# A hybrid decoder step on one core: three feature tiles at the opening, another order for the bias table's copies, wider value products and a later state store

## The chip, the core and the metric

The kernel runs on one core of one Trainium2 chip. A core has TensorE (PE, matrix products into PSUM), VectorE (DVE), ScalarE (ACT), GpSimd (POOL), and SyncE (SP), which here only issues transfers; the transfers themselves are carried by 16 DMA engines. Every engine runs its own instructions in the order in which they were written, and waits on semaphores for the others. The time is the device time of one execution in microseconds (us), given as the median of several runs.

## The reference

One layer of a decoder trunk for a prompt of 512 tokens and for 8 running sequences with one new token each. The input of 1024 columns is multiplied by one weight matrix of 3600 columns; the parts of the result feed two mixers:

```python
h = jnp.einsum('btd,de->bte', x, w_in)
qa, ka, va, za, ga, qb, kb, vb, gb = jnp.split(h, split_points, axis=-1)
log_a = jax.nn.log_sigmoid(jnp.einsum('btr,rk->btk', za, w_alpha2) + b_alpha) / GATE_TEMP
o_a, s_new = gla_chunked(qa * DK_A ** -0.5, ka, va, log_a, s0, chunk)  # S_t = diag(a_t) S_{t-1} + k_t^T v_t, o_t = q_t S_t
o_a = o_a * lax.rsqrt(jnp.mean(jnp.square(o_a), axis=-1, keepdims=True) + RMS_EPS) * gla_norm_g
o_b = prompt_dilated(qb, kb, vb, rel_bias)    # 8 heads; windows of 128, 512, 2048 at steps 1, 4, 16
mix = jnp.concatenate([o_a * jax.nn.silu(ga), o_b * jax.nn.silu(gb)], axis=-1)
x_new = layer_norm(DEEPNORM_ALPHA * x + mix @ w_out, ln_g, ln_b)
```

Mixer A (qa, ka, va, za, ga) is gated linear attention with four heads and a running state; mixer B (qb, kb, vb, gb) is attention over strided windows of keys with a bias by distance. Outputs are the new rows, the states and the new keys and values.

## The kernel before

**Precision and products.** All products of float32 numbers are made of three faster ones: each operand is split into a high part, rounded to the fast type by ScalarE (`hi`), and a rest, made by VectorE (`lo`); TensorE then adds hi·hi, hi·lo and lo·hi (`three`, lines 611 to 613). A feature tile is 128 columns of the weights against all 520 token columns, in two halves of 264 and 256, with 8 blocks of 128 rows: 48 products per tile.

**A planner writes the order.** The kernel is written as tasks (Python generators). `Plan` keeps a model of when each engine is free, with a cost for each operation (`Op`, lines 81 to 127), and always issues the operation that can start first in the model; between those that start together the task with the smaller priority number goes first (`PRIO`, line 70). The result is a fixed order of instructions on each engine. The chip then runs those orders with its own times. A transfer's cost in the model depends on its bytes, on the length of its runs and on the number of rows; all transfers that the model knows share one queue.

**Tiles.** `SLOTS` and `BANKS` name rings of buffers. The weights as loaded go into `r` (2 slots), the split weights into `w` (6 slots, so three pairs), most other things into `g` (27). PSUM has eight banks: three `d` for the feature and token products, three `s`, two `t`. A weight tile's load is issued when a slot in `r` comes free, that is when an earlier tile has been split; its split is placed as soon as a pair in `w` comes free.

**The opening** (`first_loads`, `first_splits` and the head of `dense`). The list `FIRST` (line 533) alternates blocks of x (128 rows of x, 266 KB; the first one in two halves) and blocks of the first weights, the 256 columns of ka0 and ka1. SP issues them in that order, ScalarE and VectorE split them, and TensorE multiplies block by block into four banks, so that it can work while x still arrives. Four small loads of the gate's second weights (`wz`) go over ScalarE's queue at the very start (`clear`). Behind the opening stands the product of x with the gate's first weights (`za`, line 705), and its logarithm and running sums (`gate_decay`, lines 747 to 783); then follow the features qa0, qa1, qb0 to qb3, kb0 to kb3, and on through `dense`.

**The bias table** (`bias_table`, lines 787 to 805). A product gives one row of 640 biases for each of 8 heads. The rows are stored to DRAM (`tab`), and then copied there 23 times per head into `tabr` [8, 23, 640] in one transfer from DRAM to DRAM (line 804), so that a tile of 128 rows, each shifted by one against the row above, can be read from it. These reads are the 16 `strip` loads (lines 1114 to 1127): row p of a strip is put together from two counters, 8 outer and 16 inner.

**Scores and values.** `softmax` adds the strip, makes the probabilities, turns them by TensorE and splits them; `weighted` (lines 1198 to 1226) multiplies them with the values. The value tile holds the high parts in its first 64 columns and the low parts in the next 64. For each block of keys there is one product of all 128 columns with the high probabilities, and one of the first 64 columns with the low ones.

**The levels of mixer A.** `gla_levels` (lines 808 to 855) makes, for seven block sizes, decayed copies of qa and ka (`d`, exponentials on ScalarE, `qs` and `ks` on VectorE), and `gla_level` their products (`ps_l`), two sizes together.

**The end.** The last products go to the rows of the last token block; then the state's last product, its copy by ScalarE and its store over ScalarE's queue (lines 950 to 957) stand beside the last layer norm (`norm(3)`, lines 1580 to 1615), which needs a chain of five small ScalarE steps between VectorE's statistics and its last pass over the rows.

Of the kernel before, what the change touches and what calls it, by code (L numbers as in the profile page):

```python
# [67 lines left out]


PRIO = dict(  # L70
    wload=3, wsplit=4, decay=10, res_s=8, res=8, level=22, keys_out=2, logit=50, value=20, fills=9, bias_table=7.3, gla_levels=15.3, gla_diagonal=7.7, gla_state=24, gla_queries=25, strips=14, sample_queries=48, sample_softmax=2.5, sample_values=46, sample_gla=11, mix_sample_a=8.7, mix_sample_b=16, ln_rows=17, keys_store=17.5, gla_out=26, sample_v=12, mix_tiles=33.5, scores=31, softmax=34.2, weighted=30, mix_a=18, mix_b=19, norm3=11, norm=9)
# [9 lines left out]
class Op:  # L81
# [3 lines left out]
    def __init__(self, eng, fn, args, kw):  # L85
# [13 lines left out]
        if fn == "dma_start":  # L99
            c = 640 if eng.name == "SP" else 100  # L100
# [93 lines left out]
class Plan:  # L194
# [11 lines left out]
    def pool(self, tag, n, pool):  # L206
        self.slots[tag] = [(pool, f"{tag}{i}", {}) for i in range(n)]
# [11 lines left out]
    def free(self, *xs):  # L219
        for x in xs:  # L220
            name = x.tensor.name
            self.shares[name] = self.shares.get(name, 1) - 1
            if self.shares[name] == 0:
                last = {}
                for (_, eng), end in self.uses.pop(name, {}).items():
                    last[eng] = max(last.get(eng, 0.0), end)
                tag, (pool, t, _) = self.slot_of.pop(name)
                self.slots[tag].append((pool, t, last))

    def alloc(self, need):  # L230
        for i, tag in enumerate(need.tags):
            slots = self.slots[tag]
            if len(slots) > (need.spare if i == len(need.tags) - 1 else 0):
                s = min(slots, key=lambda s: max(s[2].values(), default=0.0))
                slots.remove(s)
                pool, t, last = s
# [132 lines left out]
def trunk(ctx: ExitStack, tc: tile.TileContext, xT, xp, xs, state, ck, cv, w_in, wab, gnorm,  # L369
# [42 lines left out]
    def split(raw, hi, lo):  # L412

        yield S.copy(hi, raw)
        yield V.tensor_tensor(lo, raw, hi.bitcast(F32), op=ALU.subtract)
# [89 lines left out]
    order = [g for k, g in groups.items() if k not in ("ka0", "ka1")] + wo  # L505
# [29 lines left out]
    ka_raw = []  # L535

    def first_loads():
        za = w_in[:, OFF["za"]:OFF["za"] + 16].rearrange("(k p) n -> p k n", p=P)
        for n, a, *b in FIRST:
            if n == "x":  # L540
                c = b[0] if b else slice(0, NT)
                if a % 2 == 0 and c.start == 0:
                    xraw.append((yield Need("g", f"x_raw{a}", [P, 2, NT])))
                yield D.dma_start(xraw[a // 2][:, a % 2, c], xT[a * P:(a + 1) * P, c])
            else:
                if a % 4 == 0:
                    ka_raw.append((yield Need("r", f"raw_ka{a}", [P, 4, GW])))
                rows = w_in[a * P:b[0] * P, OFF["ka"]:OFF["ka"] + GW]
                yield D.dma_start(ka_raw[a // 4][:, a % 4:a % 4 + b[0] - a, :], rows.rearrange("(k p) n -> p k n", p=P))
            mark("first")  # L550
        yield D.dma_start(zw[:, :, :16], za)
        mark("zw")
# [8 lines left out]

    ka_hl = []

    def first_splits():
        for j, (n, a, *b) in enumerate(FIRST):
            yield At("first", j + 1)
            if n == "x":
# [6 lines left out]
                yield from split(xraw[a // 2][:, a % 2, c], xh[a][:, c], xl[a][:, c])  # L574
                mark("xs")
            else:
                if a % 4 == 0:
                    hl = []
                    for x in ("hi", "lo"):
                        hl.append((yield Need("w", f"{x}_ka{a}", [P, 4, GW], F32R)))  # L580
                    ka_hl.append(hl)
                    for i in range(2):
                        g = groups[f"ka{i}"]
                        for l, y in zip((g.hi, g.lo), hl):
                            l += [y[:, k, i * P:i * P + P] for k in range(4)]
                r = slice(a % 4, a % 4 + b[0] - a)
                yield from split(ka_raw[a // 4][:, r, :], *(y[:, r, :] for y in ka_hl[a // 4]))
                for _ in range(a, b[0]):
                    mark("kas")
                if b[0] % 4 == 0:  # L590
                    free(ka_raw[a // 4])
# [92 lines left out]
    def dense():  # L684
# [6 lines left out]
        for i in range(2):  # L691
            for u in range(2):
                pk[i, u] = yield bank("ds"[i], f"ps_ka{i}{u}")
        for k in range(KT):
            for u in range(2):
                yield At("kas", k + 1)
                yield At("xs", k + 1 + (u if k == 0 else 1))
                for i in range(2):
                    yield from three(pk[i, u][:, :TW[u]], k, halves(k, u, groups[f"ka{i}"]))
        for x in ka_hl:  # L700
            free(*x)

        pz = yield bank(("t", "s"), "ps_za")
        yield At("zw")
        yield Batch(T.matmul(pz[j * 32:j * 32 + 32, :QN[j]], zw[:, k, :], xraw[k // 2][:, k % 2, Q0[j]:Q0[j] + QN[j]],
                             start=k == 0, stop=k == KT - 1, skip_group_check=True)
                    for k in range(KT) for j in range(TT))
        free(zw, *xraw)
        add(gate_decay(pz), PRIO["decay"])
# [5 lines left out]
        for i in range(2):  # L715
            yield from feature(groups[f"qa{i}"], into("qa", qa_s, i, 0.125))
# [29 lines left out]

    def gate_decay(pz):
# [8 lines left out]
        la = yield Need("g", "la", [P, 2 * NP + 2 * NB])  # L756
# [9 lines left out]
        ls = la[:, 2 * NP:].rearrange("p (m b) -> p m b", m=2)  # L766
        parts_ = [(zv[j][:, :, :P], lv[:, :, j * P:j * P + P], lv[:, :, j * P:j * P + P]) for j in range(TT)]
        parts_.append((zv[1][:, :, P:], ls, la_s))
# [18 lines left out]
    def bias_table():  # L787
# [16 lines left out]
        yield D.dma_start(tabr, tab[:, None, :].to_broadcast([HB, T_R, T_P]))  # L804
# [97 lines left out]
    def gla_state():  # L902
# [51 lines left out]
        free(kt, B["va1"])  # L954
        yield S.copy(st[:, TT - 1].rearrange("p m v -> p (m v)"), ps[:, :256])
# [158 lines left out]
    def strips():  # L1114
        yield At("tab")
        yield At("qb", 1)
        for pi in range(2):
            w = 256 * (pi + 1)
            for h in range(HB):
# [6 lines left out]
                                                 ap=[[T_P - 16, 8], [T_P - 1, 16], [1, w]]))  # L1126
# [71 lines left out]
    def weighted(h, pi):  # L1198
# [12 lines left out]
        for k in range(last + 1):  # L1211
# [3 lines left out]
            yield T.matmul(pv[:64, o], vk[:, :64], ptl[:, k, o], start=False, stop=k == last, skip_group_check=True)  # L1215
# [364 lines left out]
    def norm(t):  # L1580
# [18 lines left out]
        if last:  # L1599
# [3 lines left out]
            yield S.activation(rstd, nt[:, 0:1], AF.Identity, scale=rstd)  # L1603
            yield from centre(cs[0])
# [20 lines left out]
    add(fills(), PRIO["fills"])  # L1625
    add(dense(), 100)
# [124 lines left out]
```

## Time and profile before

| | us |
|---|---|
| median of 3 runs | 289.97 |
| range of the runs | 289.93 to 292.68 |
| the profiled execution | 290.49 |
| its span, from the first to the last instruction | 288.6 |

The span of the profiled execution is 1.9 us shorter than its own time; what lies between is around the instructions. The busy times of the engines, the chain of waits and the rows of single instructions stand in the prediction, ahead of the sentences that use them. A row of a group reads: line, engine, operation, written tile, read tiles, shapes, count, then busy time and mean duration in ns, then the engine's idle time ahead and who ended it. All operations are recorded at one line (364, the planner's), so groups are told apart by the names of their tiles. In a row of a timeline the first number is the start, the second the duration, both in us. A row of the chain gives start, length and engine in the same way. A queue's row (SPq, ACTq) is the issue of a transfer, not its run; the transfers themselves are seen as the share of the 16 DMA engines and in GB/s.

### The profile page before, as it was taken

Reading aid. Unit: us, or ns where it says so; the run is one execution under the profiler, and the core shown is the slowest. Engines: PE = TensorE matmul, PEld = TensorE weight load, DVE = VectorE, ACT = ScalarE, POOL = GpSimd, SP = SyncE. Lnnn points to the kernel's source line nnn. Section 1 sums busy time; section 2 is a strip of 40 time slices with the busy share of each in tenths; the row PEclk is TensorE's granted clock in tenths of the full one; section 3 lists DMA queues with packets and bytes.
Section 4 is the critical chain, followed back from the end, with each engine's and each line's share of the span. In section 5 each row is a group of like instructions: output and inputs, shape, how many; then the busy total and the mean of one; then the engine's idle time right before and its main releaser. Section 6 shows DMA issues by size and latency. Waiting matters only on the chain.

```text
span 288.6 us, 6896 instructions
## 1 busy us (share of the span) xinstructions
PE 276.3 (96%) x2638; PEld 261.0 (90%) x2638; DVE 223.9 (78%) x549; ACT 168.9 (59%) x472; POOL 54.3 (19%) x74
## 2 busy tenths in 40 slices
PE   7999999999999999999999999999999969999990
PEld 4999999998999999898999999999999969997890
DVE  3837897999889879899899877756889594339845
ACT  5757564455559757585979875454899563212002
POOL 4000001000871337203124433620000000000000
PEclk9999999999999999999999999999999979999997
DMA  7976422226945897369999994765483779731112
GB/s 215 269 194 200 127 75 75 75 79 195 314 166 170 286 265 251 112 181 276 229 191 211 261 238 136 240 182 155 120 215 106 199 259 261 115 134 73 77 75 91
DMA packets 59079, 51.18 MB, mean 177 GB/s; under 512 B 12570, under 2 KB 50468, under 8 KB 59046
## 3 DMA queue, kind: packets, MB, share of 16 engines
q1 hardware_dynamic: 58522, 50.40, 61.5%
q8 instruction: 21, 0.34, 0.6%
q10 hardware_dynamic: 524, 0.34, 0.4%
q14 instruction: 12, 0.10, 0.1%
HBM read 45.17 MB, written 6.03 MB: 177 GB/s over the span
## 4 chain that ended last, share of the span: by engine, by line
PE 78%; DVE 10%; ACT 5%; DMA 4%; issue 1%; SPq 1%; DVEq 0%; ACTq 0%
PE ps_qb L364 8%; PE ps_gb L364 8%; PE ps_y L364 8%; PE ps_yf L364 8%; PE ps_kb L364 5%; PE ps_va_f L364 4%; PE ps_vb L364 4%; PE ps_qa L364 4%; PE ps_vb_f L364 4%; PE ps_va L364 4%; PE ps_pv L364 4%; PE ps_ka L364 4%; PE ps_pt L364 3%; PE ps_s L364 3%; DMA raw_wo__3535<-in_w_out_dram 2%; PE ps_l L364 1%
## 5 line engine op out<-in xcount | busy, mean ns | idle before, releaser
L364 POOL TENSOR_TENSOR vv<-vv,pb 128x256 f32<-128x256 f32 x32 | 25.1, 818 | 47.2 <-DMA pb<-psd_s 41.4
L364 POOL TENSOR_TENSOR past<-past,qbc 128x256 f32<-128x256 f32 x32 | 25.0, 812 | 43.3 <-DMA past<-in_ck_dram 42.5
L364 ACT ACTIVATE pr<-pr,ms 128x128 f32<-128x128 f32 (+3 forms) x51 | 27.0, 549 | 7.9 <-DVE ms L364 7.8
L364 DVE CUSTOM_DVE_ANT_0 pr<-ps_s,strip 128x128 f32<-128x128 f32 (+3 forms) x32 | 14.3, 477 | 1.0 <-DMA strip<-tabr 0.8
L364 PE MATMUL ps_pt<-cf,pr 128*128 128x128 f32 x80 | 14.0, 278 | 0.3 <-DVE pt L364 0.2
L364 ACT ACTIVATE sg<-sg 128x264 f32<-128x264 f32 (+1 forms) x32 | 13.4, 419 | 0.3
L364 PE MATMUL ps_ka<-xx,hi_ka 128*128 128x264 f32 (+1 forms) x64 | 12.7, 297 | 0.8 <-ACT xx L364 0.5
L364 PEld LDWEIGHTS ps_ka<-xx,hi_ka 128*128 128x128 f32 x64 | 10.4, 193 | 1.6 <-ACT xx L364 0.7
L364 ACT ACTIVATE d<-d 128x512 f32<-128x512 f32 x13 | 7.8, 635 | 6.7 <-DVE d L364 6.7
L364 PEld LDWEIGHTS ps_pt<-cf,pr 128*128 128x128 f32 x80 | 9.3, 140 | 1.3 <-DVE pt L364 0.4
L364 DVE TENSOR_TENSOR ptl<-ps_pt,pth 128x384 fp32r<-128x384 f32 (+1 forms) x16 | 9.7, 619 | 0.4 <-ACT pth L364 0.2
L364 DVE TENSOR_TENSOR obT<-ps_pv,pvl 64x256 f32<-64x256 f32 x16 | 6.5, 413 | 4.3 <-ACT pvl L364 4.1
L364 DVE TENSOR_REDUCE o_pv<-vv 128x4 f32<-128x1024 f32 x8 | 9.7, 1212 | 0.0
L364 DVE TENSOR_REDUCE lt<-past 128x16 f32<-128x1024 f32 x8 | 9.6, 1206 | 0.0
L364 ACT CAST pth<-ps_pt 128x384 fp32r<-128x384 f32 (+1 forms) x16 | 8.4, 530 | 1.7 <-PE ps_pt L364 1.6
L364 POOL MEMSET att<- 64x512 f32 x2 | 1.0, 520 | 44.1 <-DVE ks L364 44.1
L364 PE MATMUL ps_ka<-xx,lo_ka 128*128 128x264 f32 (+1 forms) x32 | 9.1, 283 | 0.0
L364 DVE TENSOR_TENSOR xx<-x_raw,xx 128x520 fp32r<-128x520 f32 (+2 forms) x9 | 5.8, 640 | 4.1 <-ACT xx L364 4.0
L364 ACT COPY feat_y<-ps_yf 128x256 f32<-128x256 f32 x7 | 2.6, 373 | 10.7 <-PE ps_yf L364 10.7
L364 DVE TENSOR_TENSOR d<-b 128x1024 f32<-128x1024 f32 x7 | 8.5, 1216 | 0.0
L364 PE MATMUL ps_s<-kp,qh 64*128 64x128 f32 (+3 forms) x64 | 8.3, 345 | 0.0
L364 ACT COPY pvl<-ps_pv 64x256 f32<-64x256 f32 x16 | 5.7, 368 | 4.1 <-PE ps_pv L364 3.5
(540 smaller groups left out, 1092.9 us busy)
## 6 DMA issues: line engine op xcount, KB each, us to landing
past<-in_ck_dram SPq DMA_DIRECT2D x8, 512.0 KB
vv<-in_cv_dram SPq DMA_DIRECT2D x8, 512.0 KB
pb<-psd_s SPq DMA_DIRECT2D x16, 256.0 KB
qbc<-qsd SPq DMA_DIRECT2D x8, 256.0 KB
strip<-tabr SPq DMA_DIRECT2D x8, 256.0 KB
y<-in_xp_dram SPq DMA_DIRECT2D x4, 512.0 KB
x_raw<-in_xT_dram SPq DMA_DIRECT2D x7, 260.0 KB
out_dram<-y SPq DMA_DIRECT2D x3, 512.0 KB
```

Source lines behind the costliest of these rows:

```text
L364: getattr(eng.eng, op.fn)(*op.args, **op.kw)
```

## The change

It has these parts.

- **Opening.** Three feature tiles instead of two: ka0, ka1 and qa1, whose columns lie side by side in the weights. They take six banks, all of `d` and `s`. Each weight block is now 128 rows of 384 columns (196 KB) and is loaded alone; the first one in two pieces, of which the first (ka0 and ka1) goes over ScalarE's queue, the second (qa1) over SP. The first weight piece is rounded by VectorE instead of ScalarE, and the rest of the first half of x is made between that and the rest of the weights.
- **Gate.** The four wz loads go over SP's queue behind the opening's loads. The za product becomes a task of its own (`gate_ranks`) with priority 48.3, where it stood in the line of `dense`; `gate_decay` belongs to it. The sample's log-decay is made in its own small tile.
- **Bias table.** The copy into `tabr` runs over the 23 copies outermost and the heads inside them; the table in DRAM is laid out as before. A strip's row counters are 16 outer and 8 inner; the same data are read.
- **Values.** The product with the low probabilities takes all 128 columns, except for the last block of keys of a unit. What it adds in columns 64 to 127 is low times low parts.
- **State.** The copy of the state's last product and its store wait until the five ScalarE steps of `norm(3)` are placed.
- **Planner.** Two of the four probability tiles have room for 384 columns instead of 512 (`ROOMS`), and the smallest that fits is taken. A transfer issued by ScalarE costs 400 ns in the model, not 100. Other priorities: logit 25.7 (was 50), gla_levels 7.6 (15.3), sample_softmax 8.7 (2.5), sample_v 9.2 (12).

```diff
-            c = 640 if eng.name == "SP" else 100
+            c = 640 if eng.name == "SP" else 400
...
+ROOMS = dict(pr=[512] * 2 + [384] * 2)
...
-    order = [g for k, g in groups.items() if k not in ("ka0", "ka1")] + wo
+    first = [groups[n] for n in ("ka0", "ka1", "qa1")]
+    FW, FO = 3 * P, OFF["qa"] + P
+    order = [g for g in groups.values() if g not in first] + wo
...
-        for j in range(4):
-            yield S.dma_start(wz[j * 32:j * 32 + 18], wab[80:98])
-    FIRST = (("x", 0, TS[0]), ("w", 0, 1), ("x", 0, TS[1]), ("w", 1, 2), ("x", 1), ("w", 2, 4), ("x", 2), ("x", 3),
-             ("w", 4, 6), ("x", 4), ("x", 5), ("w", 6, 8), ("x", 6), ("x", 7))
+    FIRST = (("x", 0, TS[0]), ("w", 0, slice(P, FW)), ("x", 0, TS[1]), ("w", 0, slice(0, P)), ("w", 1), ("x", 1),
+             ("w", 2), ("x", 2), ("w", 3), ("x", 3), ("w", 4), ("x", 4), ("w", 5), ("x", 5), ("w", 6), ("x", 6), ("w", 7), ("x", 7))
...
+                yield (S if a == 0 and c.start else D).dma_start(first_raw[a // 2][:, a % 2, c], w_in[a * P:(a + 1) * P, FO + c.start:FO + c.stop])
             mark("first")
         yield D.dma_start(zw[:, :, :16], za)
+        for j in range(4):
+            yield D.dma_start(wz[j * 32:j * 32 + 18], wab[80:98])
...
-        for i in range(2):
+        for i in range(3):
             for u in range(2):
-                pk[i, u] = yield bank("ds"[i], f"ps_ka{i}{u}")
+                pk[i, u] = yield bank(("d", "s"), f"ps_first{i}{u}")
         for k in range(KT):
-            for u in range(2):
-                yield At("kas", k + 1)
-                yield At("xs", k + 1 + (u if k == 0 else 1))
-                for i in range(2):
-                    yield from three(pk[i, u][:, :TW[u]], k, halves(k, u, groups[f"ka{i}"]))
+            for i in ((0, 1), (2,)) if k == 0 else ((0, 1, 2),):
+                for u in range(2):
+                    yield At("firsts", k + 2 if k else 1 if 0 in i else 2)
+                    yield At("xs", k + 1 + (u if k == 0 else 1))
+                    for j in i:
+                        yield from three(pk[j, u][:, :TW[u]], k, halves(k, u, first[j]))
...
+    def gate_ranks():
+        yield At("zw")
+        yield At("first", len(FIRST))
+        pz = yield bank("t", "ps_za")
+        yield Batch(T.matmul(pz[j * 32:j * 32 + 32, :QN[j]], zw[:, k, :], xraw[k // 2][:, k % 2, Q0[j]:Q0[j] + QN[j]],
+                             start=k == 0, stop=k == KT - 1, skip_group_check=True)
+                    for k in range(KT) for j in range(TT))
+        free(zw, *xraw)
+        yield from gate_decay(pz)
...
-        yield D.dma_start(tabr, tab[:, None, :].to_broadcast([HB, T_R, T_P]))
+        yield D.dma_start(tabr.rearrange("h r t -> r h t"), tab[None, :, :].to_broadcast([T_R, HB, T_P]))
...
-                                                 ap=[[T_P - 16, 8], [T_P - 1, 16], [1, w]]))
+                                                 ap=[[T_P - 8, 16], [T_P - 1, 8], [1, w]]))
...
+        yield At("last")
         yield S.copy(st[:, TT - 1].rearrange("p m v -> p (m v)"), ps[:, :256])
...
-            yield T.matmul(pv[:64, o], vk[:, :64], ptl[:, k, o], start=False, stop=k == last, skip_group_check=True)
+            if k < last:
+                yield T.matmul(pv[:, o], vk, ptl[:, k, o], start=False, stop=False, skip_group_check=True)
+            else:
+                yield T.matmul(pv[:64, o], vk[:, :64], ptl[:, k, o], start=False, stop=True, skip_group_check=True)
```

More of the change, by code (lines that the diff above doesn't have):

```diff
@@ L206, in pool @@
     def pool(self, tag, n, pool):
-        self.slots[tag] = [(pool, f"{tag}{i}", {}) for i in range(n)]
+        self.slots[tag] = [(pool, f"{tag}{i}", {}, r) for i, r in zip(range(n), ROOMS.get(tag, [0] * n))]
     def add(self, gen, prio):
@@ L226, in free @@
                     last[eng] = max(last.get(eng, 0.0), end)
[L227 to L228 removed]
+                tag, (pool, t, _, room) = self.slot_of.pop(name)
+                self.slots[tag].append((pool, t, last, room))
     def alloc(self, need):
@@ L232, in alloc @@
             slots = self.slots[tag]
-            if len(slots) > (need.spare if i == len(need.tags) - 1 else 0):
-                s = min(slots, key=lambda s: max(s[2].values(), default=0.0))
+            n = math.prod(need.shape[1:]) if tag in ROOMS else 0
+            fits = [s for s in slots if s[3] >= n]
+            if fits and len(slots) > (need.spare if i == len(need.tags) - 1 else 0):
+                s = min(fits, key=lambda s: (s[3], max(s[2].values(), default=0.0)))
                 slots.remove(s)
-                pool, t, last = s
+                pool, t, last, _ = s
                 x = pool.tile(need.shape, need.dt, name=need.name, tag=t)
@@ L410, in copy, with split @@
         return V.tensor_copy(o, x), S.copy(o, x)
-    def split(raw, hi, lo):
-        yield S.copy(hi, raw)
+    def split(raw, hi, lo, eng=None, rest=()):
+        yield V.tensor_copy(hi, raw) if eng is V else S.copy(hi, raw)
+        yield from rest
         yield V.tensor_tensor(lo, raw, hi.bitcast(F32), op=ALU.subtract)
@@ L690, in dense @@
         pk = {}
-        for i in range(2):
+        for i in range(3):
             for u in range(2):
-                pk[i, u] = yield bank("ds"[i], f"ps_ka{i}{u}")
+                pk[i, u] = yield bank(("d", "s"), f"ps_first{i}{u}")
         for k in range(KT):
-            for u in range(2):
-                yield At("kas", k + 1)
-                yield At("xs", k + 1 + (u if k == 0 else 1))
-                for i in range(2):
-                    yield from three(pk[i, u][:, :TW[u]], k, halves(k, u, groups[f"ka{i}"]))
-        for x in ka_hl:
-            free(*x)
[L703 to L709, printed above, removed]
+            for i in ((0, 1), (2,)) if k == 0 else ((0, 1, 2),):
[4 more added lines that the diff above has]
+                        yield from three(pk[j, u][:, :TW[u]], k, halves(k, u, first[j]))
+        for x in first_hl:
+            free(*x)
         yield from make("ka", Need("g", "ka", [P, 2, NP]), 3)
@@ L714, in dense @@
                 add(into("ka", ka_s, i, 1.0)(pk[i, u], u), 2)
-        for i in range(2):
-            yield from feature(groups[f"qa{i}"], into("qa", qa_s, i, 0.125))
+        for u in range(2):
+            add(into("qa", qa_s, 1, 0.125)(pk[2, u], u), 2)
+        yield from feature(groups["qa0"], into("qa", qa_s, 0, 0.125))
         for x in ("qh0", "ql0", "qh1", "ql1"):
@@ L1603, in norm @@
             yield S.activation(rstd, nt[:, 0:1], AF.Identity, scale=rstd)
+            mark("last")
             yield from centre(cs[0])
@@ L1625, in trunk @@
     add(fills(), PRIO["fills"])
+    add(gate_ranks(), PRIO["decay"])
     add(dense(), 100)
```

48 lines of the change are left out of this document (26 added, 22 removed).

## The prediction

> **What bounds the kernel now.** I read the page first (engine totals, then the 40 slices), then the waits of TensorE, then the chain of waits in order of time, and last the timelines of single queues where the change touches them.
>
> ```profile
> PE 276.3 (96%) x2638; PEld 261.0 (90%) x2638; DVE 223.9 (78%) x549; ACT 168.9 (59%) x472; POOL 54.3 (19%) x74
> ...
> PE 78%; DVE 10%; ACT 5%; DMA 4%; issue 1%; SPq 1%; DVEq 0%; ACTq 0%
> ```
>
> The reader is to see an engine that is already full: PE is busy for 96% of the span and carries 78% of the chain. An edit that takes work off another engine can give something only where PE waits. Its waits on other engines are few; these are the longest behind the warm-up:
>
> ```profile
> PE ps_yf L364 <- DVE ga L364: 2.5, 1, 2.5
> PE ps_ka L364 <- ACT xx L364: 0.5, 1, 0.5
> PE ps_ka L364 <- DVE xx L364: 0.3, 1, 0.3
> ```
>
> So there are three places to win: the opening (before 7.6 us), one wait of 2.5 us, and the tail after the last product. To lose there is everything in between, since PE, VectorE and ScalarE each run their instructions in a written order, and whoever is stopped stops the others:
>
> ```profile
> 38.00:70.00 32.00, 31.73 (x611) 30.63 (x609) 29.60 (x46) 15.97 (x32) 1.04 (x2) 1.00 0.29 80
> 230.00:240.00 10.00, 7.46 (x49) 7.24 (x48) 7.50 (x18) 5.91 (x15) 0.00 (x0) 0.83 0.74 244
> ```
>
> (Columns: stretch, length, busy us of PE, PEld, DVE, ACT, POOL, granted clock, DMA share, GB/s.) From 38 to 70 us VectorE is busy for 29.6 of 32 us, so time that it loses there it doesn't get back.
>
> **The change part by part.** The sum is made against the profiled execution: 290.49 us, of which the span is 288.6. The median of the runs is 289.97, 0.5 below it.
>
> *Opening.* Before, two feature tiles (ka0, ka1) are made while x arrives; after, three (with qa1).
>
> ```profile
> 4.23 0.98 PE L364 MATMUL ps_ka<-xx,hi_ka 128*128 128x264 f32 x2
> ...
> 6.87 0.39 PE L364 MATMUL ps_ka<-xx,hi_ka 128*128 128x264 f32 x1 [0.45 <-ACT xx L364]
> 7.61 0.39 PE L364 MATMUL ps_ka<-xx,hi_ka 128*128 128x264 f32 x1 [0.34 <-DVE xx L364]
> ```
>
> ```profile
> 7.61 10.32 PE ps_ka L364 x83
> ```
>
> ```profile
> 2.60 0.43 SPq L364 DMA_DIRECT2D x_raw<-in_xT_dram  x1
> ```
>
> Of the 96 products, 83 run from 7.61 on, at 10.32/83 = 0.124 us, without a gap; 13 are done before. What stops PE is the second block of x, issued at 2.60 as SP's fifth transfer. It stays the fifth, because the first weights go to ScalarE's queue. Ahead of it now lie 130 KB more weights (three tiles' rows instead of two, twice) and 72 KB fewer of wz, some 0.2 to 0.4 us. In the time until then PE now has 18 products of the first block, not 12: five or six more by 0.124 are 0.6 to 0.7 us. Net I take -0.4; the ends are -1.4 (the first product also comes earlier, through the second queue and VectorE's copy, and all PE idle of these rows goes) and +0.6 (all six banks of the rings d and s are taken, so qa0 waits for an evacuation). The qa1 work itself is only moved: 48 products cost the same at 0.124 there.
>
> *The gate's product, its logarithms and the new priorities.* The za and z products stay on PE; they may only stand elsewhere, and the four wz loads pass from ScalarE's queue to SP's. The decay's ScalarE and VectorE steps are the same ones. The cover is the products of qa0 and qb0, which PE makes meanwhile; were it gone, the first level product would come late by what the decay is late. The decay's first banks come free only behind the opening, but qa, which the levels need too, is complete one tile earlier. 0, ends -1.5 and +1.5.
>
> *Smaller probability tiles* (two of 512, two of 384): the later query blocks need exactly two of each. 0.
>
> *Strips on more engines.* VectorE's only wait for a strip is 0.8 us, and PE has none for it:
>
> ```profile
> L364 DVE CUSTOM_DVE_ANT_0 pr<-ps_s,strip 128x128 f32<-128x128 f32 (+3 forms) x32 | 14.3, 477 | 1.0 <-DMA strip<-tabr 0.8
> ```
>
> 0, ends -0.8 and 0.
>
> *Value products without a change of mode.* The low halves' products get 128 columns instead of 64, except the last.
>
> ```profile
> 134.73 0.28 PE L364 MATMUL ps_pv<-ptl,vhl 128*64 128x256 f32 x1
> 134.85 0.28 PE L364 MATMUL ps_pv<-pth,vhl 128*128 128x256 f32 x1
> ...
> 135.20 0.33 PE L364 MATMUL ps_pv<-pth,vhl 128*128 128x256 f32 x1
> 135.46 0.62 PE L364 MATMUL ps_s<-kp,qh 64*128 64x384 f32 x4
> ```
>
> Starts of neighbours lie 0.12 us apart whether the tile is 128 or 64 columns wide: nothing is lost in the change and nothing can be won. I take 0. A change of rows does cost: 135.20 to 135.46 is 0.26, 0.14 more. The Trainium skill says otherwise of columns too (TensorEngine Tiling (Array Packing), Key Properties: a change of the tiling mode drains the TensorE); this case's trace disagrees for 128 to 64 columns. By that rule the 64 changes that go (2 in each of 8 early units, 6 in each of 8 late ones) would give 64 x 0.14 = 9 us.
>
> *State store later.* The copy and the store of the state stand between the last VectorE statistics and ScalarE's chain of five.
>
> ```profile
> 281.84 0.26 DVE L364 BATCH_NORM_AGGREGATE mv<-stats 128x2 f32<-128x24 f32 x1
> 281.95 0.37 ACT L364 COPY st_all<-ps_kv 128x256 f32<-128x256 f32 x1 [9.90 <-PE ps_kv L364]
> 282.22 0.30 ACT L364 ACTIVATE rstd<-mv,eps 128x1 f32<-128x1 f32 x1
> 282.36 0.43 ACTq L364 DMA_DIRECT2D out_dram<-st_all  x1
> 282.83 0.20 ACT L364 ACTIVATE rstd<-rstd 128x1 f32<-128x1 f32 x1 [0.32 <-ACT rstd L364]
> 284.05 1.54 DVE L364 SCALAR_TENSOR_TENSOR y<-y,rstd,beta 128x512 f32<-128x512 f32 x3 [0.43 <-ACT rstd L364]
> ```
>
> The issue at 282.36 holds the chain for 0.32, the copy for 0.1 more; VectorE waits 0.43 at its end. So -0.4, ends -0.43 and 0; the store itself then runs beside the last stores of y.
>
> *The table's copy.* This is the term that decides. The bias table is written out 23 times per head (471 KB) from DRAM to DRAM. Before, its outermost dimension is the 8 heads; after, the 23 copies.
>
> ```profile
> 1.45 1.70 ACTq L364 DMA_DIRECT2D wz<-in_wab_dram  x4
> ...
> 23.54 0.78 SPq L364 DMA_DIRECT2D tabr<-tab  x1
> 26.75 0.37 SPq L364 DMA_DIRECT2D raw_qb__438<-in_w_in_dram  x1
> 29.50 0.37 SPq L364 DMA_DIRECT2D raw_qb__473<-in_w_in_dram  x1
> ```
>
> ```profile
> 21.00:22.00 1.00, 1.00 (x19) 0.88 (x20) 0.18 (x1) 1.00 (x2) 0.00 (x0) 1.00 1.07 317
> 26.60:27.60 1.00, 1.00 (x11) 1.00 (x10) 0.97 (x4) 0.70 (x2) 0.00 (x0) 1.00 0.49 182
> ```
>
> While a weight load of 128 rows runs (21 to 22 us), the 16 DMA engines are full: share 1.07. While the table's copy runs alone (26.6 to 27.6) half are: 0.49, at 182 GB/s. Eight heads, eight engines, 22.8 GB/s each. So a copy is dealt out by its outermost dimension, and I read the half share as equal portions. 23 is prime: no number of engines from 2 to 16 gets equal portions of it, and I take one engine. Then the copy lasts 471/22.8 = 20.7 us. The ends: 16 engines (1.3 us) and one. The Trainium skill (DMA: Bandwidth & Descriptors, Why a DMA increments its semaphore by 16 and not by 1) states it so: the engines used are the largest number up to 16 that divides the slowest dimension of both sides. By that rule, too, it is one engine here, and the trace's 8 for 8 agrees with it; no run so far has 23.
>
> What waits behind it: the loads of qb2 and qb3 take all 16 engines, this one included, and stand behind the copy on the same queue; that they wait for it on its engine is what I take, since nothing in the rows lets one of SP's transfers overtake another. Issue of the copy: 23.54 plus four wz issues on SP (1.70 on ScalarE's queue) plus 0.3 for three more transfers in the opening, 25.5 (between 23.5, if SP's waits hide all of that, and 27). In the row of 26.6 the copy is running some 3 us behind its issue, but after the end of a weight load; I take 1.2: data from 26.7 to 47.4; the two loads add 512 KB/317 GB/s = 1.65 us each: qb3 is there at 50.7, whichever of them goes first.
>
> ```profile
> 32.94 1.04 ACT L364 CAST hi_qb__530<-raw_qb__438 128x1024 fp32r<-128x1024 f32 x1
> ...
> 39.23 1.05 ACT L364 CAST hi_qb__614<-raw_qb__473 128x1024 fp32r<-128x1024 f32 x1 [1.07 <-PE ps_qb L364]
> 40.18 0.38 ACT L364 ACTIVATE qh<-ps_qb 128x256 fp32r<-128x256 f32 x1
> 40.76 1.15 ACT L364 ACTIVATE d<-d 128x512 f32<-128x512 f32 x2 [0.20 <-DVE d L364]
> ```
>
> ```profile
> 43.04 0.68 DVE L364 TENSOR_TENSOR ks<-ka,d 128x512 f32<-128x512 f32 x1
> ```
>
> ```profile
> 44.59 2.00 PE ps_l L364 x128
> ```
>
> The planner knows nothing of it (its cost of a copy hangs on bytes, not on engines), so the split of qb3 keeps its place on ScalarE, as soon as qb0's slot is free: 39.23, in the new kernel 0.4 earlier, 38.8. There ScalarE waits until 50.7, 11.9 us. Behind it stand the evacuation of qb0 and the exponentials of the second level, behind those ks on VectorE, and behind that PE's level products, with 44.59 - 43.72 = 0.9 us to spare. PE so loses 11.9 - 0.9 = 11.0 us. The ends: 9.0 if the copy is issued as early as before (two us less); 15 if qb2's load also falls behind it, since its split stands at 32.94 and ScalarE then stops from there to 49; and 1.7 more if the clock falls as in the row of 230 to 240 us (10 x (1 - 0.83)).
>
> Sum: 290.5 - 0.4 - 0.4 + 11.0 = 300.7, less 0.5 to the median: 300.2 us. The likeliest case's own range: 290.0 - 1.8 + 9.0 = 297.2 to 290.0 - 0.8 + 16.7 = 306.
>
> **The rivals.**
>
> *The copy hinders nobody.* If it runs on three engines or more, it ends by 26.7 + 20.7/3 = 33.6, qb3 is there at 36.9, before its place at 38.8, and the whole term is nought: 290.0 - 0.8 = 289.2, no change that can be told. The same follows if the loads pass the copy on its engine. For it: no row shows that 23 can't be dealt out unequally, and none shows a load behind an unfinished copy. Against it: the half share of 8. It decides from three engines upward.
>
> *The wait at 230 us closes* (the other side: faster). Given the first rival, the new order of priorities could bring forward the evacuation of ps_ga for which PE waits 2.5 us, after which the clock is 0.83 for 10 us (1.7 lost): 289.2 - 4.2 = 285.0. For it: ScalarE and VectorE are 59 and 75% busy there, so the order matters. Against it: no edit moves that work itself. Under 287.1 it counts as faster, so it needs half of the 4.2.
>
> *Mode changes cost after all*: 289.2 - 9 = 280. The rows at 134.7 to 135 speak against it; 0.02.
>
> **How the numbers follow.** A measurement of this kernel can tell about 1% from no change. The table's copy stops the opening's successors: 0.55, and it is slower than 292.9 with all its ends. Of the 0.45 left, 0.23 go to no change (the first rival with the ends of the small terms) and 0.22 to faster (0.20 the wait, 0.02 the modes). The range for 8 in 10 is 286 to 305: below it lie some 0.12, of the fast cases, above it some 0.06, where the ends 15 and 1.7 come together.
>
> **What would show it.** Copy on one engine: a stretch of about 20 us from 27 us on with a DMA share near 0.06, and ScalarE idle some 12 us (or 17) on the DMA of qb's weights, PE idle about 11 us between 38 and 55. Opening: three tiles' products from before 4.2 on, PE's idle at 6.9 to 7.6 smaller. Tail: the chain of five without the 0.32. Value products: 0.12 us apart as before. The forecast is wrong if the qb weights land before 38 us; then the copy ran on three engines or more, or the loads passed it.

## The result and the profile after

| | before | after |
|---|---|---|
| median, us | 289.72 (6 runs, 287.83 to 292.68) | 298.08 (6 runs, 296.54 to 298.52) |
| ratio, 95% interval | | 1.030 [1.0255, 1.0343], slower |
| the profiled execution, us | 290.49 | 296.54 |
| its span, us | 288.6 | 294.8 |

Ratios, here and below, leave out executions more than 1.5% above the fastest of their kernel, such as the 292.68. The profiled execution of the kernel after is the fastest of its six, so what is read in it is rather a little less than the whole loss: the two executions with a mean granted clock of 0.985 and 0.986 took 296.5 and 296.8 us, the three with 0.975 to 0.977 took 298.3 to 298.5. First its page: the engine totals, three rows of the 40 slices (7.4 us each), and the shares of the chain of waits.

```profile
PE 277.1 (94%) x2638; PEld 261.5 (89%) x2638; DVE 223.6 (76%) x546; ACT 171.9 (58%) x481; POOL 59.7 (20%) x74
...
PE   8999999279999999999999999989999999999991
...
PEclk9999999969999999999999999999999999999998
DMA  6963404243853969652989867876467498761112
...
PE 56%; DVE 16%; ACT 13%; DMA 11%; issue 2%; SPq 1%; DVEq 0%; ACTq 0%
```

TensorE is busy for 0.8 us more than before and idle for 17.7 us instead of 12.3. The hole is in one place, the eighth slice (digit 2), and the clock dips in the slice behind it (digit 6). DMA has taken 11% of the chain, where it had 4%. The waits of TensorE name the place:

```profile
PE ps_l L368 <- DVE ks L368: 7.0, 1, 7.0
PE warm_ps L368 <- DVE warm L1640: 1.2, 1, 1.2
PE ps_va_f L368 <- DVE lo_va__2973 L368: 1.0, 1, 1.0
```

There is one wait of 7.0 us, for the level products. The wait of 2.5 us for `ga` is no longer in the list. VectorE is named, but VectorE had itself been stopped; the chain of waits, in order of time, leads back to what held all three engines:

```profile
35.04 19.72 DMA raw_kb__547<-in_w_in_dram
54.76 0.02 issue
54.79 1.05 ACT hi_kb__683 L368
55.84 0.02 issue
55.86 1.22 DVE lo_kb__684 L368
57.09 1.14 DVE d L368
...
59.93 0.69 DVE ks L368
60.62 0.04 issue
60.67 1.93 PE ps_l L368 x64
```

A load of 512 KB is on its way for 19.72 us; qb3's, as large and issued at 31.01, takes 3.8. SP's timeline shows what was issued just ahead of it, and ScalarE's shows how long that engine stood:

```profile
27.28 0.37 SPq L368 DMA_DIRECT2D raw_qb__445<-in_w_in_dram  x1
27.74 0.43 SPq L368 DMA_DIRECT2D tab<-tsb  x1
31.01 0.37 SPq L368 DMA_DIRECT2D raw_qb__491<-in_w_in_dram  x1
31.47 0.73 SPq L368 DMA_DIRECT2D tabr<-tab  x1
35.04 8.64 SPq L368 DMA_DIRECT2D raw_kb__547<-in_w_in_dram  x1
43.78 6.22 SPq L368 DMA_DIRECT2D raw_kb__628<-in_w_in_dram  x1
```

```profile
45.08 0.36 ACT L368 ACTIVATE qh<-ps_qb 128x256 fp32r<-128x256 f32 x1
54.79 1.04 ACT L368 CAST hi_kb__683<-raw_kb__547 128x1024 fp32r<-128x1024 f32 x1 [9.34 <-DMA raw_kb__547<-in_w_in_dram]
```

The copy of the table is issued at 31.47, and the two loads behind it are kb0 and kb1, not qb2 and qb3, which stand ahead of it. The windows show what the DMA engines did meanwhile, and what the pause cost the clock (columns as in the prediction):

```profile
36.00:44.00 8.00, 8.00 (x70) 8.00 (x69) 6.93 (x15) 4.79 (x15) 0.00 (x0) 1.00 0.08 29
...
57.00:61.00 4.00, 0.33 (x12) 0.34 (x16) 3.08 (x6) 2.41 (x5) 0.00 (x0) 0.56 0.48 131
61.00:65.00 4.00, 4.00 (x74) 3.94 (x71) 3.93 (x7) 1.44 (x4) 0.00 (x0) 0.58 0.45 125
65.00:69.00 4.00, 4.00 (x36) 4.00 (x35) 3.59 (x6) 2.09 (x5) 0.00 (x0) 1.00 0.05 11
```

From 36 to 44 us the share is 0.08, near 1/16: one engine of sixteen works. Behind the pause the granted clock is 0.58 until 65 us, which costs 4 x 0.42 = 1.7 us.

The trace keeps a record of each portion of a transfer that lands. In the copies of fewer than 16 portions there is also one record 1.1 to 1.3 us after the issue, some 2 us or more ahead of the first portion. I read it as no portion; without it the portions of the table's copy are:

```
kernel                     outermost  portions  issued   last landing  us
before                      8          8         23.54    29.93         6.4
after                      23          1         31.47    53.26        21.8
e1_heads_outside            8          8         32.10    38.65         6.6
e2_copies_outside_before   23          1         23.92    45.66        21.7
e3_25_copies               25          5         32.03    40.35         8.3
e4_scalar_queue            23          1         32.94    57.52        24.6
e5_29_copies               29          1         31.69    58.36        26.7
e6_24_copies               24         12         31.46    37.12         5.7
e12_16_and_7               16 and 7   16 and 7   31.67    36.49         4.8
```

The lower rows belong to the experiments.

### The profile page after: what moved, and what is told of

It is laid out like the page before. It is cut to its first block, busy times and chain, and to the rows that moved or that the text cites. A ratio compares the mean times of both kernels' runs of the same rounds, so it can differ in the third digit from the quotient of the medians.

```text
span 294.8 us, 6902 instructions
## 1 busy us (share of the span) xinstructions
PE 277.1 (94%) x2638; PEld 261.5 (89%) x2638; DVE 223.6 (76%) x546; ACT 171.9 (58%) x481; POOL 59.7 (20%) x74
## 4 chain that ended last, share of the span: by engine, by line
PE 56%; DVE 16%; ACT 13%; DMA 11%; issue 2%; SPq 1%; DVEq 0%; ACTq 0%
PE ps_y L368 8%; PE ps_yf L368 7%; DMA raw_kb__547<-in_w_in_dram 7%; PE ps_gb L368 6%; PE ps_first L368 5%; PE ps_vb_f L368 4%; PE ps_vb L368 4%; PE ps_va L368 3%; PE ps_pv L368 3%; ACT pr L368 3%; PE ps_pt L368 3%; PE ps_qb L368 2%; ACT sg L368 2%; PE ps_qa L368 2%; PE ps_s L368 2%; DMA past<-in_ck_dram 2%
## 5 line engine op out<-in xcount | busy, mean ns | idle before, releaser
L368 POOL TENSOR_TENSOR past<-past,qbc 128x256 f32<-128x256 f32 x32 | 29.1, 946 | 87.3 <-DMA past<-in_ck_dram 87.3
L368 POOL TENSOR_TENSOR vv<-vv,pb 128x256 f32<-128x256 f32 x32 | 26.4, 855 | 47.0 <-DMA pb<-psd_s 45.0
L368 ACT ACTIVATE pr<-pr,ms 128x128 f32<-128x128 f32 (+3 forms) x59 | 30.8, 547 | 4.3 <-DVE ms L368 4.2
L368 PE MATMUL ps_first<-xx,hi_first 128*128 128x264 f32 (+1 forms) x96 | 18.8, 296 | 0.1
L368 PEld LDWEIGHTS ps_first<-xx,hi_first 128*128 128x128 f32 x96 | 15.7, 197 | 0.9 <-DVE xx L368 0.4
L368 PE MATMUL ps_l<-qs,ks 64*64 64x32 f32 (+1 forms) x352 | 7.6, 233 | 7.0 <-DVE ks L368 7.0
L368 PE MATMUL ps_first<-xx,lo_first 128*128 128x264 f32 (+1 forms) x48 | 13.8, 288 | 0.0
L368 PEld LDWEIGHTS ps_l<-qs,ks 64*64 64x64 f32 x352 | 7.0, 150 | 7.7 <-DVE ks L368 7.1
L368 ACT ACTIVATE rstd<-mv,eps 128x1 f32<-128x1 f32 x4 | 1.1, 291 | 18.6 <-DVE mv L368 18.6
L368 PEld LDWEIGHTS ps_first<-xx,lo_first 128*128 128x128 f32 x48 | 9.4, 196 | 0.0
```

The source lines that it names most:

```text
L368: getattr(eng.eng, op.fn)(*op.args, **op.kw)
```

## The experiments

All times are medians; ratios are to the kernel before, run on the same chip. "The changed kernel" is the kernel after.

### The copy alone, out of the change and into the kernel before

`e1_heads_outside`: the changed kernel, with one line as it was.

```diff
-        yield D.dma_start(tabr.rearrange("h r t -> r h t"), tab[None, :, :].to_broadcast([T_R, HB, T_P]))
+        yield D.dma_start(tabr, tab[:, None, :].to_broadcast([HB, T_R, T_P]))
```

> The changed kernel, with the table's copy over the 8 heads outermost again; all other parts stay. Theory E (one engine): the copy falls from 21.8 us to 6 to 7, kb0 lands by 40 us instead of 54.8, ScalarE's idle of 9.3 us and PE's wait of 7.0 us go, and the clock keeps 1.00 from 38 to 61 us (1.8 us more): 298.1 - 7.0 - 1.8 = 289.3, at most 1.5 to either side. Rival P (the new order of priorities, with the running sums 10 us later, is the cause): the wait stays in another place, 295 to 298 us.

Measured: 288.06 us, ratio 0.9962 [0.9929, 0.9995]. TensorE's wait at the level products is gone, kb0 lands at 40.62, and ScalarE goes on without a pause (its timeline, for comparison with the rows above, and the level products in the chain of waits):

```profile
45.72 0.36 ACT L368 ACTIVATE qh<-ps_qb 128x256 fp32r<-128x256 f32 x1
45.98 1.04 ACT L368 CAST hi_kb__683<-raw_kb__547 128x1024 fp32r<-128x1024 f32 x1
```

```profile
53.24 2.00 PE ps_l L368 x128
```

The order of instructions on TensorE, ScalarE and SP is the same as in the changed kernel; only the shape of the one transfer differs. So the copy's outermost dimension costs 1.0299/0.9962 = 1.034, some 9.8 us, and the rest of the change gives 0.4%, with an interval from nearly nothing to 0.7%. Rival P falls: the last running sum starts as late here (at 42.8 us, against 42.1 in the changed kernel and 32.3 before), and TensorE doesn't wait for it.

`e2_copies_outside_before`: the kernel before, with the opposite edit.

> The kernel before, with only the table's copy over the 23 copies outermost. Here the loads of qb2 and qb3 are issued behind the copy (26.75 and 29.50 against 23.54 us). Theory E: the copy lands at 23.5 + 21.8 = 45.3, qb2 at about 47, ScalarE stops at its split from 33 to 47 and PE loses 11 to 14 us plus up to 1.8 of clock: 301 to 305 us. Rival P (the copy alone does nothing): 289 to 291. Rival F (only a load that is issued within some microseconds of the copy's end waits): 295 to 298.

Measured: 302.36 us, ratio 1.0469 [1.0398, 1.054], +13.6 us; rivals P and F fall. Here the loads that wait are qb2 and qb3. ScalarE's timeline, and TensorE's longest wait:

```profile
33.03 0.38 ACT L364 ACTIVATE qa<-ps_qa 128x256 f32<-128x256 f32 x1 [1.18 <-PE ps_qa L364]
47.31 1.04 ACT L364 CAST hi_qb__530<-raw_qb__438 128x1024 fp32r<-128x1024 f32 x1 [13.89 <-DMA raw_qb__438<-in_w_in_dram]
```

```profile
PE ps_qb L364 <- ACT q_s L364: 8.7, 1, 8.7
```

TensorE's wait is less than the 11 to 14 us expected; this profile, too, is of the fastest execution (300.23). The same copy costs 9.8 us in one order and 13.6 in the other. That the difference lies in which load stands behind it, and how soon that load is needed, fits the waits (ScalarE 9.34 and 13.89, TensorE 7.0 and 8.7).

### How the copy is dealt out

`e3_25_copies`, `e6_24_copies`: the changed kernel with another number of rows per head; the additional rows are written and never read.

```diff
-T_R = 23
+T_R = 25   # e3; 24 in e6, 29 in e5
```

> The changed kernel with 25 rows of copies per head instead of 23 (two more than are read, 9% more bytes). Theory E with equal portions: 25 = 5 x 5, so 5 engines, 512 KB / (5 x 22) = 4.7 us and some 2 us of start; landing 7 us behind its issue, kb0 there by 41 us, 289 to 291 us. Rival G (any outermost dimension that is not the old one of 8 goes to one engine, as its rows are scattered): 23.6 us, 298 to 300. Rival H (unequal portions, and 23 was slow for its layout in DRAM, not for its engines): the number of engines at the end is 16 and the copy is as slow as with 23, 297 to 299.

> The changed kernel with 24 rows of copies per head (one is never read), 24 outermost. Theory E with equal portions on the largest number of engines up to 16: 12 engines, two rows each, 12 portions that land; 491 KB / (12 x 21.6) = 1.9 us of data, landing some 5.5 us behind the issue: 288 us, as with the heads outermost, to 0.7 either side. Rival (8 engines, three rows each): 8 portions, 2.8 us of data, landing 6.5 us behind. Rival G (one engine): 298 to 300.

Measured: 25 rows 288.1 us, ratio 0.9968 [0.9941, 0.9996], 5 portions, kb0 there at 41.76, both a little off what was expected (289 to 291 us, by 41); 24 rows 287.79 us, ratio 0.9954 [0.992, 0.9987], 12 portions, kb0 there at 39.60. Rivals G and H fall, and so does the rival of 8 engines for 24 rows. The counts of all runs, 16 for 16 rows, 7 for 7, 8 for 8, 12 for 24, 5 for 25 and one for 23 and for 29, are the largest divisor up to 16. That is the rule of the Trainium skill (DMA: Bandwidth & Descriptors, Why a DMA increments its semaphore by 16 and not by 1), and these runs agree with it in every case. Two rows more, and 9% more bytes, made the copy of the table 2.6 times as fast (8.3 us instead of 21.8).

`e5_29_copies`: another prime, so a longer copy on the same single engine.

> The changed kernel with 29 rows of copies per head (the last six are never read), 29 outermost: a prime again, so one engine by theory E, with 594 KB instead of 471. At the rate of the changed kernel, 471 / 21.8 = 21.6 KB a microsecond, it lasts 27.5 us; kb0 lands 5.7 us later, at 60.5, PE's wait at the level products grows from 7.0 to 12.7 us: 298.1 + 5.7 = 303.8, from 302.5 to 305. Rival N (the loss comes from SP's blocked issues or from the start of such a copy, not from its length): 297 to 299.

Measured: 302.22 us (301.40 to 304.16), ratio 1.0452 [1.04, 1.0505]. TensorE's waits:

```profile
PE ps_l L368 <- DVE ks L368: 11.9, 1, 11.9
```

The copy takes 4.88 us more and the wait grows by 4.9: one for one. Rival N falls by its time and by its claim that the length doesn't count. The run doesn't part the length of the copy from SP's blocked issue, which grows as much (8.64 to 13.52 us); `e4_scalar_queue` does. The median is just under the range given, 1.6 us under its middle. Half of that (5.7 - 4.9 = 0.8) is that I had taken the whole 21.8 us as proportional to the bytes; the rest is open. Six rows are 6 x 8 x 2560 B = 123 KB in 4.88 us, 25.2 KB a microsecond; of the 21.8, 471/25.2 = 18.7 are data and 3.1 are there whatever the length (an estimate from two copies).

`e12_16_and_7`: the changed kernel with the copy cut in two, so that nothing is written in vain.

```diff
-        yield D.dma_start(tabr.rearrange("h r t -> r h t"), tab[None, :, :].to_broadcast([T_R, HB, T_P]))
+        for r, n in ((0, 16), (16, T_R - 16)):
+            yield D.dma_start(tabr.rearrange("h r t -> r h t")[r:r + n], tab[None, :, :].to_broadcast([n, HB, T_P]))
```

> The changed kernel with the copy in two transfers, 16 rows and 7 rows, each with the rows outermost; nothing is written that isn't read. The planner counts one transfer more, and so places some instructions otherwise. Theory E with equal portions: 16 portions of the first and 7 of the second, kb0 there by 41 us, no wait of PE at the level products: 287.5 to 289.5. Rival (the other placement costs by itself): the copy lands as early, but PE waits elsewhere, 290 to 294.

Measured: 288.26 us, ratio 0.9958 [0.9923, 0.9993]; kb0 is there at 39.10, TensorE has no wait at the level products. A shorter copy gains nothing further: with 5, 8, 12 or 16 engines kb0 lands between 39.1 and 41.8, and its split stands at 45.98 (row of `e1_heads_outside`).

### Does the load wait for the engine or for the queue?

`e4_scalar_queue`: the changed kernel, with the copy issued by ScalarE instead of SP.

```diff
-        yield D.dma_start(tabr.rearrange("h r t -> r h t"), tab[None, :, :].to_broadcast([T_R, HB, T_P]))
+        yield S.dma_start(tabr.rearrange("h r t -> r h t"), tab[None, :, :].to_broadcast([T_R, HB, T_P]))
```

> The changed kernel, with the same copy of 23 outermost, but issued over ScalarE's queue, where it stands behind the split of qb2 (32.5 us). The loads of the weights stay on SP's. Theory Q (a load waits for what is ahead of it in its own queue on that engine; two queues share an engine in turns): the copy still takes 20 us or more, but kb0 lands by 42 us and PE loses at most 1 us: 289 to 291. Rival R (an engine works off whatever came first, from all queues): kb0 lands at 55 to 57 us and the time stays at 297 to 300.

Measured: 291.89 us, ratio 1.011 [1.0077, 1.0142]. It lies between the two expectations: the loads are neither free nor held until the copy's end. TensorE is full from 38 to 61 us (23.00 of 23), as in `e1_heads_outside`; it loses 3.5 us from 61 to 126 (60.84 busy against 64.34), most of it in three waits of 0.8 to 1.3 us between 62 and 75. The chain of waits leads from there back over VectorE to kb1's load, 14.25 us on its way. ScalarE's timeline:

```profile
48.04 1.05 ACT L368 CAST hi_kb__683<-raw_kb__546 128x1024 fp32r<-128x1024 f32 x1 [2.03 <-DMA raw_kb__546<-in_w_in_dram]
...
56.03 1.05 ACT L368 CAST hi_kb__751<-raw_kb__628 128x1024 fp32r<-128x1024 f32 x1 [2.96 <-DMA raw_kb__628<-in_w_in_dram]
```

The portions of the loads, from the same records:

```
                     issued   SP held for   portions 1 to 15 land   portion 16 lands
after, kb0           35.04    8.64          46.54 to 46.85          54.76
after, kb1           43.78    6.22          52.75 to 53.20          56.25
e4, kb0              35.60    0.37          38.88 to 39.28          48.02
e4, kb1              41.70    0.37          45.00 to 45.35          55.95
```

Two effects are told apart here. On its own queue the copy holds even the issue: SP needs 8.64 us to give out kb0, and so the fifteen portions on idle engines come late as well, and kb1's issue later still. (What the held issue adds to the loss by itself isn't shown: kb0's sixteenth portion, on the copy's engine, comes last in any case, 1.5 us behind the copy's end.) From another queue the issue is free and fifteen portions land after 3.3 us, but the sixteenth shares its engine with the copy and lands 9 us behind the others. Theory Q was right in kind (turns, not first come first served) and wrong in the size of a turn. Between the landings of the two sixteenth portions lie 7.93 us for 512/16 = 32 KB, which the engine alone would carry in 32.8/25.2 = 1.3 us. In the other 6.6 us the copy moves 167 KB, five times as much. Five is also the ratio of the runs, 2560 B of the copy to 512 B of the load. That fits turns counted in runs and not in bytes; it is an estimate, at the 25.2 KB a microsecond found above, and no run with other sizes shows it. The Trainium skill (DMA: Bandwidth & Descriptors, Queues, rings and completion order) has each engine go round its queues packet by packet, a packet being several descriptors; the trace agrees that there are turns, and doesn't show the packets.

### The other parts, each taken back alone

All three stand on `e1_heads_outside`, so that the copy is out of the way.

`e7_values_64`:

```diff
-            if k < last:
-                yield T.matmul(pv[:, o], vk, ptl[:, k, o], start=False, stop=False, skip_group_check=True)
-            else:
-                yield T.matmul(pv[:64, o], vk[:, :64], ptl[:, k, o], start=False, stop=True, skip_group_check=True)
+            yield T.matmul(pv[:64, o], vk[:, :64], ptl[:, k, o], start=False, stop=k == last, skip_group_check=True)
```

> The copy over the heads outermost (as in e1_heads_outside), and the low halves' value products 64 columns wide again, as in the kernel before. The view of neighbours' starts, 0.12 us apart whatever the width: no difference to e1_heads_outside, 288.1, to 0.8 either side. Rival (a change of 128 to 64 columns drains TensorE, 0.14 us at each of 64 changes): 297.

Measured: 287.76 us, ratio 0.9968 [0.9942, 0.9995], against 0.9962. No difference; the 9 us of the rival are excluded.

`e10_strips_8`:

```diff
-                                                 ap=[[T_P - 8, 16], [T_P - 1, 8], [1, w]]))
+                                                 ap=[[T_P - 16, 8], [T_P - 1, 16], [1, w]]))
```

> The copy over the heads outermost (as in e1_heads_outside), and the strip loads with the row counters of the kernel before, 8 outer. The order of all instructions is that of e1_heads_outside. The strips land on 8 engines instead of 16, later by some us; VectorE's waits for strips come to 0.8 to 2 us, PE has none: 288.1 to 288.9. Rival (the strips hold up scores): over 290.

Measured: 287.44 us, ratio 0.9944 [0.9909, 0.9979]. No difference to 0.9962, and less than expected. The strips land on 8 engines here and on 16 there; the first six take 3.1 to 7.5 us and 2.6 to 7.5. VectorE waits for a strip in neither, where I had expected 0.8 to 2 us: the layout of before alone doesn't make the 0.8 us in its profile.

`e11_state_early`:

```diff
-        yield At("last")
```

> The copy over the heads outermost (as in e1_heads_outside), and the copy and the store of the state where the planner puts them without a condition. The chain of five on ScalarE gets its break of 0.3 us back, the span grows by 0.4 us: 288.1 to 288.9, which the runs can hardly tell; the timeline at the end tells it. Rival (the store then collides with the stores of y, or nothing waits for the chain): 287.7 to 288.1, VectorE's wait for rstd nought.

Measured: 287.99 us, ratio 0.998 [0.995, 1.0011]; the time can't tell. VectorE's timeline at the end can, first with the early store, then with the late one:

```profile
279.34 0.26 DVE L368 BATCH_NORM_AGGREGATE mv<-stats 128x2 f32<-128x24 f32 x1
...
281.52 1.54 DVE L368 SCALAR_TENSOR_TENSOR y<-y,rstd,beta 128x512 f32<-128x512 f32 x3 [0.41 <-ACT rstd L368]
```

```profile
279.72 0.26 DVE L368 BATCH_NORM_AGGREGATE mv<-stats 128x2 f32<-128x24 f32 x1
...
281.56 1.54 DVE L368 SCALAR_TENSOR_TENSOR y<-y,rstd,beta 128x512 f32<-128x512 f32 x3
```

From the statistics to the last pass 2.18 us with the early store, 1.84 with the late one (`e1_heads_outside`): the state's later place gives 0.34 us.

### The priorities

`e8_old_priorities`: `e1_heads_outside` with the whole line `PRIO` of the kernel before. `e9_priorities_before`: the kernel before with the new line, decay 48.3 for 10 among it.

```diff
-    wload=3, wsplit=4, decay=48.3, ... logit=25.7, ... gla_levels=7.6, ... sample_softmax=8.7, ... sample_v=9.2, ...
+    wload=3, wsplit=4, decay=10, ... logit=50, ... gla_levels=15.3, ... sample_softmax=2.5, ... sample_v=12, ...
```

> The copy over the heads outermost (as in e1_heads_outside), and all priorities of the kernel before; the three tiles of the opening and the rest stay. Theory W (the new priorities closed the wait at 230 us): PE waits some 2.5 us for ga again and the clock falls there, up to 4.2 us: 290.5 to 292.3. Rival (the wait closed through the shifted opening, or it is not worth its length): 287.5 to 288.7.

> The kernel before, with only the new priorities; the copy stays over the heads outermost, the opening has two tiles. Theory J (priorities and opening fit only together, as the old priorities cost 7.3 us with the new opening): waits of PE appear elsewhere, some us longer than the kernel before, 291 to 297 us. Rival W (the new priorities close the wait at 230 us by themselves): that wait of up to 2.5 us and its clock loss of 1.7 go, 285 to 288.

Measured: the old priorities with the new opening 295.37 us, ratio 1.0204 [1.0157, 1.0252] (a loss, though the interval doesn't tell whether it is over 2%), by the ratios 7.0 us more than `e1_heads_outside` and outside both expectations; the new priorities with the old opening 290.08 us, ratio 1.0046 [1.0005, 1.0088]. In `e8_old_priorities` theory W has only the smaller part of the loss. The waits of TensorE, and then the windows of the two places:

```profile
PE ps_gb L368 <- DVE gb L368: 3.5, 1, 3.5
PE ps_yf L368 <- ACT hi_wo__3725 L368: 1.8, 1, 1.8
```

```profile
155.00:170.00 15.00, 11.50 (x76) 10.70 (x75) 13.33 (x33) 9.07 (x23) 3.84 (x5) 0.77 0.77 210
...
228.00:248.00 20.00, 17.77 (x152) 16.65 (x151) 14.31 (x32) 11.57 (x30) 0.00 (x0) 0.91 0.72 229
```

The wait for the first `ps_yf` is back, at 242 us in this kernel, now on the weights' split (1.8 and 0.3 us), with a clock of 0.91 over 20 us. The larger loss is a new one: 3.5 us until 164.0, with a clock of 0.77 over 15 us. In `e9_priorities_before` the wait at 230 is closed, and still the kernel isn't faster: a new loss of 1.6 us stands between 155 and 170, where the kernel before is full.

```profile
155.00:170.00 15.00, 13.38 (x111) 12.60 (x112) 14.07 (x35) 10.66 (x29) 4.92 (x7) 1.00 1.06 217
225.00:240.00 15.00, 14.58 (x121) 14.22 (x120) 11.91 (x26) 9.61 (x26) 0.00 (x0) 1.00 0.80 258
```

So the new priorities do close that wait, with either opening, as rival W had it for `e9_priorities_before`; but its time of 285 to 288 fell. Theory J holds in kind, though its 291 to 297 was too much. Each of these two orders opens a wait somewhere else in the 290 us, and where is seen only in the trace.

## Why the prediction was right, and where not

**The direction and the copy.** The time, 298.1, lies 2.1 below the 300.2 predicted. The decisive step, that half the DMA share for 8 heads means equal portions and that 23 copies therefore go to one engine, is borne out by all seven numbers tried: 7, 8, 16, 23, 24, 25 and 29. From issue to landing the copy was put at 1.2 + 20.7 = 21.9 us and took 21.8. The parts were otherwise, by the estimate above 3.1 and 18.7: the rate from the half share, 22.8 GB/s, stands between the 25.2 of the data alone and the 21.6 over all, and its error and that of the start cancelled by luck.

**Which load waits: wrong.** The prediction put the issue at 25.5 us, from SP's row alone: its old place, four more issues, 0.3 for the opening. It was at 31.47, outside the span of 23.5 to 27. What sets it is TensorE's product of the table, which follows the opening. The view of that tile, before and after:

```profile
L364 PE MATMUL ps_tab<-ct,rb x1: 402/402/402, 19.8 to 19.8; 66*8 66x512 f32 x1
```

```profile
L368 PE MATMUL ps_tab<-ct,rb x1: 391/391/391, 26.5 to 26.5; 66*8 66x512 f32 x1
```

With a third tile in the opening the product comes 6.7 us later, the store of the table with it (27.74), and the copy must wait for that store's landing (31.37). It is the opening that does it: with three tiles and the old priorities the copy is issued at 31.46 (`e8_old_priorities`), with two tiles and the new ones at 24.01 (`e9_priorities_before`). So qb2 and qb3 went ahead, and kb0 and kb1 stood behind. The prediction followed the moved step on SP's queue and not back to its producer. By the sign that it had named, qb's weights there before 38 us, it was wrong: they landed at 31.2 and 34.8. But neither reason that it gave for that sign held, more engines or loads that pass the copy. That another pair of loads stood behind the copy, and held ScalarE nearly as long, was luck.

**What the wait costs: the sum nearly right, its terms not.** Predicted: ScalarE stops for 11.9 us, TensorE loses 11.0, the clock nothing (1.7 was kept as an end). Measured: ScalarE 9.34, TensorE 7.0 in the wait, since with kb0 there are 2.3 us to spare instead of 0.9, and the clock about 2: TensorE is busy 277.1 us instead of the 274.9 of `e1_heads_outside`, of which 1.7 from 61 to 65 us alone. Between the medians of these two lie 10.0 us, since the clock was lower in most other executions of the kernel after than in the profiled one; if the wait is 7.0 in them too, the clock and what else differs come to some 3. Too large a wait and a clock left out of the sum partly cancelled, which was luck. The pause of 7.0 us can't be priced without the clock behind it; the 1.7 kept as an end belonged in the sum.

**The small terms.** *Opening, -0.4:* take from each trace the start of the k-th of the opening's products (counted from 0), less k x 0.1235 us, and the latest of these for k from 10 to 60. It says from when an unbroken row of products would have had to run. The three traces with two tiles give 6.16, 6.53 and 6.62 us, the eleven with three tiles 5.70 to 6.35, on the mean 6.44 and 6.01: 0.43 us, with a spread between executions that is larger. *Tail, -0.4:* 0.34. *Value products, 0:* right; the trace and now a run (0.9968 against 0.9962) disagree with the Trainium skill (TensorEngine Tiling (Array Packing), Key Properties) for a change from 128 to 64 columns. *Strips, 0:* right. *Priorities, 0:* right for the change as a whole, since opening and priorities came together; taken apart, the new ones gain 7.0 us with the new opening, far beyond the ends of 1.5 that I gave, and lose 1.3 with the old one. The cover that I named held: the levels come 8.7 us later in `e1_heads_outside` than before (53.24 against 44.59) and TensorE has other products meanwhile. All of it together was put at -0.8; `e1_heads_outside` shows -1.1 us [-2.1, -0.1].

**The rivals.** *The copy hinders nobody* fell, by 23 and 29; its point of decision, three engines, is borne out as far as 5 engines are enough; 2, 3 and 4 weren't tried. *The wait at 230 us closes* came true, also in the kernel after, and didn't give the 4.2 us that I had put on it. The price was read in an execution that isn't typical: on the four chips of the experiments 23 of 89 executions of the kernel before have a mean clock of 0.987 to 0.990, as the profiled one (0.988), and a median of 291.3 us; the other 66 have 0.992 or more, and 288.7. (Three of 336 to 536 us aren't counted.) That the dip at 230 us is what the 23 have in common is likely but not shown, as there is no second profile of that kernel. *Mode changes* fell.

## What to carry to other kernels

Look at the outermost dimension of every transfer as a number to be divided: what is its largest divisor up to 16? A prime above 16, like the 23 and 29 here, puts everything on one engine, and the transfers that pay most are those behind it on the same queue (9.8 us here, and still 3.8 with the copy on another queue). And when a step moves, follow its producer too, not only the queue that issues it. Then price the pause with the clock that follows it.

## What the runs showed of the hardware that was not expected

A copy on one engine stops the issue of later transfers of its queue: SP's issue of kb0 took 8.64 us behind 23 rows, 13.52 behind 29; it took 0.37 to 0.40 where the copy ran on 5, 8, 12 or 16 engines, and 0.37 where it was on another queue. A load is done only with its last portion: with the copy on ScalarE's queue fifteen of sixteen portions of kb0 landed at 39.3 and the last at 48.0.
